# Rotating the sparse queries and keys: rows swapped by transfers within SBUF in place of a product with a permutation matrix

## The chip, the cores and the metric

The kernel runs on one core of a Trainium2 chip. The metric is the device time of one execution in microseconds (us), median over runs. Engines: PE is TensorE, DVE is VectorE, ACT is ScalarE, POOL is GpSimd, SP only issues transfers. Each engine works off its own queue in order, and engines wait for each other through semaphores.

## What is computed

A batch of 512 rows of width 1024 passes through two layers. The change lies in the second layer's sparse attention, whose heads are rotated in their first 16 of 64 dimensions:

```python
def partial_rope(x, cos, sin):
    xr = x[..., :ROT_DIM].astype(jnp.float32)
    x1, x2 = xr[..., :ROT_DIM // 2], xr[..., ROT_DIM // 2:]
    rot = jnp.concatenate([x1 * cos - x2 * sin, x2 * cos + x1 * sin], axis=-1)
    return jnp.concatenate([rot.astype(x.dtype), x[..., ROT_DIM:]], axis=-1)
...
    q = partial_rope(q.reshape(bsz, seq, A_HEADS, HEAD_DIM), cos, sin)
    k = partial_rope(k[:, :, None, :], cos, sin)[:, :, 0]
    qi = partial_rope(qi.reshape(bsz, seq, IDX_HEADS, IDX_DIM), cos, sin)
    ki = partial_rope(ki[:, :, None, :], cos, sin)[:, :, 0]
    a_out = dsa_attention(q, k, v, qi, ki, wi)
```

The index queries and keys (qi, ki) give a score for each pair of query and key; the top 128 keys of each query are kept, and softmax attention of the eight real heads (q, k, v) runs over those. Beside it in the same stage runs a convolution branch (four blocks of channels, 31 taps, layer norm). Then follow an output projection, cross attention and a feed-forward part.

## The kernel before

Every large product keeps single precision by splitting each operand into a high and a low part and adding three products (lines 385 to 387). A weight unit of 128 columns is loaded by SP into `raw`, its high part is cast on ACT (`whi`, line 361), its low part is subtracted on DVE in two halves (`wlo`, line 364), and PE then runs 24 products of 512 columns on it into a `ps_mm` buffer in PSUM, of which there are two. Three units fit into SBUF at a time.

Activations stand transposed: 128 head dimensions (two heads of 64) on the partitions, 512 rows along the free side. `roped_2` rotates such a tile: ACT copies it out of PSUM into `rx` (line 1527), PE multiplies `rx` by a constant permutation matrix `perm2` that exchanges rows 0 to 7 with rows 8 to 15 of each head (line 1529), DVE multiplies `rx` by the cosines (line 1530) and the permuted tile by the signed sines into `ry` (line 1532), adds both (line 1533), and `split` writes high and low part (`hl`, lines 409 and 410). `rx` and `ry` come from one ring of three buffers (tag `t2`), which other steps of the stage use too.

It is called eight times in `mix_2`, the stage of the change. First in `sparse_in`: index queries 0 and 1, and the index key (64 rows). From these PE computes the index scores (`scores_pair`, line 1518), ACT and DVE combine them into `acc` (lines 1486 to 1493), and DVE then runs the top-k: 48 rounds of MAX8 and MATCH_REPLACE8 (lines 1575 and 1576), each round on what the last one left. Meanwhile PE goes on with the units of the convolution branch (`conv_in`: pairs ua, ug), the convolution itself (line 1695), the key and value unit (`sparse_kv`, second rotation of 64 rows) and the four query units q0 to q3 (`sparse_q`, four rotations). The last part is `sparse_attend`: in steps of (block of 128 rows, pair of heads) PE does scores (line 1518), ACT exponentials (line 1606), PE transposes (line 1616) and products with the values (line 1629). Step (0, 0) needs q0, (0, 2) q1, (0, 4) q2 and (0, 6) q3; steps from (1, 0) on also need the masks of the top-k.

A scheduler that has its own estimate of every duration sets the order of each engine's queue from the order in which the program is written and from what would be ready. Only in `sparse_attend` with the end of the convolution branch is PE's order kept as written. So a change of one step moves others.

The first layer already has a rotation by transfers: `swap` (line 1501) exchanges halves of 32 rows with four transfers of 64 KB that ACT issues.

Of the kernel before, what the change touches and what calls it, by code (L numbers as in the profile page):

```python
# [20 lines left out]
F32 = mybir.dt.float32  # L21
# [3 lines left out]
OP = mybir.AluOpType  # L25
# [14 lines left out]
def _constants():  # L40
    p = np.arange(128)
    f = lambda a: np.asarray(a, np.float32)
    cols = {}

    def put(name, a):
        cols[name] = f(a).reshape(128, -1)

    put("ident", np.eye(128))
    put("i32", (p % 32)[:, None] == np.arange(32)[None, :])
    s, t = (p % 64)[:, None], np.arange(64)[None, :]  # L50
    put("maskS", np.concatenate([-f(t > s), t >= s], 1))
    put("maskY", np.broadcast_to((np.arange(128)[:, None] % 64) >= 32, (128, 32)))
    i, j = p[:, None], np.arange(128)[None, :]
    put("swm", np.concatenate([np.where(j > i, 0.0, NEG), np.where(j <= i, 0.0, NEG)], 1))
    put("bones", (i // 64) == (j // 64))
    put("hone", (i // 64) == np.arange(2)[None, :])
    m = p % 64
    put("perm2", (i == np.where(m < 8, p + 8, np.where(m < 16, p - 8, -1))[None, :]))
    h = np.arange(32, dtype=np.float32) / np.float32(32)
    inv1 = np.power(np.float32(10000.0), -h).astype(np.float32)  # L60
    g = np.arange(0, 16, 2, dtype=np.float32) / np.float32(16)
    inv2 = np.power(np.float32(500000.0), -g).astype(np.float32)
    put("inv", np.broadcast_to(np.concatenate([inv1, inv2]), (128, 40)))
    put("sgn1", np.where(m < 32, -1.0, 1.0))
    put("sgn2", np.where(m < 8, -1.0, np.where(m < 16, 1.0, 0.0)))
    put("rot2", m < 16)
    put("pass2", m >= 16)
    rm = np.ones((128, 8, 65))
    rm[:, :, 0] = 0
    put("rmask", rm)  # L70
    at, n = {}, 0
    order = [k for k in cols if k not in LATE] + [k for k in cols if k in LATE]
    for k in order:
        at[k] = (n, n + cols[k].shape[1])
        n += cols[k].shape[1]
    return at, np.ascontiguousarray(np.concatenate([cols[k] for k in order], 1))


LATE = ("maskS", "maskY", "bones", "rmask")
CAT, CONST = _constants()  # L80
NKEEP = CAT["maskS"][0]

# [148 lines left out]

PASS = 0.64

FILL = 32


class Builder:
# [20 lines left out]
    def setup_1(self):  # L258
        nc, I, cp = self.nc, self.I, self.cp
        self.mhalf = cp.tile([128, 16], F32, name="mhalf")  # L260
        nc.vector.memset(self.mhalf, -0.5)
        cp.tile([128, FILL], F32, name="fill")
        self.cst = cp.tile([128, NKEEP], F32, name="cst")
# [1257 lines left out]
    def roped_2(self, p, dst, ps, n, rows=None):  # L1521

        nc, V = self.nc, self.nc.vector
        C2, S2 = self.rot2
        rows = rows or 128
        x = p.tile([128, 512], F32, name="rx2", tag="t2", bufs=self.t2n)
        nc.scalar.copy(x[:rows], ps[:rows])
        pp = self.psum("at")
        nc.tensor.matmul(pp[:n], self.c("perm2")[:n, :n], x[:n], start=True, stop=True)
        V.tensor_tensor(x[:n], x[:n], C2[:n], op=OP.mult)  # L1530
        t = p.tile([128, 512], F32, name="ry2", tag="t2", bufs=self.t2n)
        V.tensor_tensor(t[:n], pp[:n], S2[:n], op=OP.mult)
        V.tensor_tensor(t[:n], x[:n], t[:n], op=OP.add)
        self.split(dst[0][:n], dst[1][:n], t[:n])
        return x
# [428 lines left out]
```

## Time and profile before

| | us |
|---|---|
| median of 3 runs | 1451.52 |
| lowest, highest | 1449.52, 1459.29 |
| the profiled execution's own time | 1450.54 |
| its span in the trace | 1448.8 |
| PE busy | 1407.9 (97%) |
| DVE busy | 870.5 (60%) |
| ACT busy | 557.9 (39%) |

The span runs from the first to the last recorded instruction; the execution's own time lies 1.7 us above it. Busy time of PE is modelled, since products overlap, and a busy PE may still run at the lower of its two clocks. The stage of the change lies between about 730 and 912 us of the span.

### The profile page before, as it was taken

The page shows a single profiled execution, that of the slowest core. Times are in us where ns is not written, and L with a number is a line of the kernel's source. Part 1 is how long each engine was busy: PE and PEld are TensorE (multiplying, and loading weights), DVE is VectorE, ACT ScalarE, POOL GpSimd, SP SyncE. Part 2 cuts the span into 40 slices and gives each one's busy share as a digit, 9 for nine tenths or more (in the row PEclk, how much of TensorE's full clock was granted, in tenths as well). Part 3 has the DMA queues.
Part 4 walks back from the last instruction along what each step waited for, and adds up shares of the span by engine and source line. Part 5 has one row for each costly group of instructions (what it writes and reads, how often), then busy time and mean ns, then how long its engine had stood idle before and what let it go on. Part 6 is the DMA issues. An engine that isn't in the chain of part 4 may idle for free.

```text
span 1448.8 us, 20320 instructions
## 1 busy us (share of the span) xinstructions
PE 1407.9 (97%) x7876; PEld 1113.7 (77%) x7876; DVE 870.5 (60%) x1983; ACT 557.9 (39%) x964; POOL 89.7 (6%) x164
## 2 busy tenths in 40 slices
PE   8799999999999999999999999999999999999998
PEld 6688768876776887887867556888888888888886
DVE  4768567776756775347569957465465555554232
ACT  4534345444344322333432126443344334343122
POOL 1101011201001000000001100000000000000000
PEclk9999999999999999999999998999999999999999
DMA  8367314422222441325226510252122332332221
GB/s 277 119 187 224 106 39 122 122 61 81 74 73 67 138 131 60 123 69 187 66 66 158 133 59 1 74 190 87 59 88 88 106 99 88 105 99 102 102 87 73
DMA packets 143617, 151.65 MB, mean 105 GB/s; under 512 B 22305, under 2 KB 118945, under 8 KB 143009
## 3 DMA queue, kind: packets, MB, share of 16 engines
q1 hardware_dynamic: 129088, 124.93, 27.6%
q0 software_dynamic: 4480, 14.98, 3.8%
q10 hardware_dynamic: 9952, 10.45, 2.2%
q8 instruction: 62, 1.02, 0.3%
q14 instruction: 35, 0.28, 0.1%
HBM read 135.33 MB, written 13.18 MB: 103 GB/s over the span
## 4 chain that ended last, share of the span: by engine, by line
PE 77%; DVE 8%; issue 2%; ACT 1%; POOL 1%; DMA 1%; ACTq 0%; POOLq 0%; DVEq 0%; SPq 0%
PE ps_mm L385 17%; PE ps_mm L386 17%; PE ps_mm L387 16%; DVE acc L1576 2%; PE ps_at L385 2%; PE ps_rw L385 2%; PE ps_at L387 2%; PE ps_at L386 2%; PE ps_rw L387 2%; PE ps_rw L386 2%; DVE m L1575 2%; DVE wlo L364 1%; PE ps_po L643 1%; PE ps_at L1518 1%; PE ps_at L614 1%
## 5 line engine op out<-in xcount | busy, mean ns | idle before, releaser
L364 DVE TENSOR_TENSOR wlo<-raw,whi 128x512 fp32r<-128x512 f32 x412 | 272.7, 683 | 279.4 <-ACT whi L361 276.1
L361 ACT CAST whi<-raw 128x1024 fp32r<-128x1024 f32 (+1 forms) x206 | 215.9, 1049 | 454.1 <-PE ps_mm L386 247.6
L386 PE MATMUL ps_mm<-blo,whi 128*128 128x512 f32 (+2 forms) x544 | 208.9, 384 | 0.0
L385 PE MATMUL ps_mm<-bhi,whi 128*128 128x512 f32 (+2 forms) x544 | 208.3, 383 | 0.0
L387 PE MATMUL ps_mm<-bhi,wlo 128*128 128x512 f32 (+2 forms) x544 | 207.6, 382 | 0.0
L385 PE MATMUL ps_mm<-hhi,whi 128*128 128x512 f32 (+1 forms) x488 | 195.2, 400 | 0.2 <-ACT hhi L409 0.2
L386 PE MATMUL ps_mm<-hlo,whi 128*128 128x512 f32 (+1 forms) x488 | 192.4, 394 | 0.8 <-DVE hlo L410 0.8
L387 PE MATMUL ps_mm<-hhi,wlo 128*128 128x512 f32 (+1 forms) x488 | 192.4, 394 | 0.0
L386 PEld LDWEIGHTS ps_mm<-blo,whi 128*128 128x128 f32 (+1 forms) x544 | 102.1, 188 | 22.9 <-issue 3.3
L385 PEld LDWEIGHTS ps_mm<-bhi,whi 128*128 128x128 f32 (+1 forms) x544 | 102.0, 188 | 21.5 <-issue 1.8
L387 PEld LDWEIGHTS ps_mm<-bhi,wlo 128*128 128x128 f32 (+1 forms) x544 | 102.0, 188 | 21.4 <-issue 1.8
L385 PEld LDWEIGHTS ps_mm<-hhi,whi 128*128 128x128 f32 x488 | 92.7, 190 | 20.4 <-issue 3.4
L387 PEld LDWEIGHTS ps_mm<-hhi,wlo 128*128 128x128 f32 x488 | 92.8, 190 | 18.2 <-issue 1.8
L386 PEld LDWEIGHTS ps_mm<-hlo,whi 128*128 128x128 f32 x488 | 92.7, 190 | 17.7 <-DVE hlo L410 1.3
L995 DVE TENSOR_TENSOR tmp<-U,L 32x31 f32<-32x31 f32 (+30 forms) x124 | 37.9, 306 | 4.2 <-DMA L<-lspill 2.0
L385 PE MATMUL ps_mm<-yhi,whi 128*128 128x512 f32 x96 | 39.1, 409 | 0.5 <-DVE ga L1183 0.3
L997 DVE TENSOR_TENSOR U<-U,tmp 32x31 f32<-32x31 f32 (+30 forms) x124 | 38.0, 306 | 2.3
L386 PE MATMUL ps_mm<-ylo,whi 128*128 128x512 f32 x96 | 38.7, 404 | 0.0
L387 PE MATMUL ps_mm<-yhi,wlo 128*128 128x512 f32 x96 | 38.3, 399 | 0.0
L421 ACT ACTIVATE nxs<-x 128x1024 f32<-128x1024 f32 x16 | 17.0, 1060 | 32.3 <-DVE x L1210 28.7
L1695 PE MATMUL ps_yk<-R,diag 128*32 128x512 f32 x256 | 29.3, 594 | 0.0
L385 PE MATMUL ps_mm<-mT,whi 128*128 128x256 f32 x96 | 28.0, 291 | 0.7 <-DVE kvt L410 0.6
(478 smaller groups left out, 2629.4 us busy)
## 6 DMA issues: line engine op xcount, KB each, us to landing
raw<-in_w_in_dram SPq DMA_DIRECT2D x24, 1024.0 KB, 5.3
raw<-in_w_in_dram SPq DMA_DIRECT2D x26, 512.0 KB, 3.9
raw<-in_w_gate_dram SPq DMA_DIRECT2D x11, 1024.0 KB, 5.1
raw<-in_w_up_dram SPq DMA_DIRECT2D x11, 1024.0 KB, 5.1
raw<-in_w_down_dram SPq DMA_DIRECT2D x10, 1024.0 KB, 4.9
raw<-in_w_out_dram SPq DMA_DIRECT2D x8, 1024.0 KB, 4.9
R<-cspill POOLq DMA_DIRECT2D x16, 270.0 KB, 6.0
raw<-in_w_k_cross_dram SPq DMA_DIRECT2D x4, 1024.0 KB, 7.8
```

The costliest lines, as they stand in the source:

```text
L361: nc.scalar.copy(h, v)
L364: self.last_lo = nc.vector.tensor_tensor(l[:, x], v[:, x], h[:, x].bitcast(F32), op=OP.subtract)
L385: mm(ps, L[0], R[0], start=first, stop=False)
L386: mm(ps, L[0], R[1], start=False, stop=False)
L387: mm(ps, L[1], R[0], start=False, stop=last)
L421: nc.scalar.activation(sc, x, AF.Square, accum_out=ss[:, 0:1])
L614: mm(pv[r][:, :n], q[64 * r:64 * r + 64, tb * 128:(tb + 1) * 128], kT[64 * r:64 * r + 64, key0:key0 + n], start=True, stop=True)
L995: V.tensor_tensor(t, U32[:np_, 0:a, m:m + 1].to_broadcast([np_, a, w]), L32[m // 16][:np_, m % 16:m % 16 + 1, m + 1:32].to_broadcast([np_, ...
L997: V.tensor_tensor(U32[:np_, 0:a, m + 1:32], U32[:np_, 0:a, m + 1:32], t, op=OP.add)
L1575: V.max(m, acc[tb][:, :n])
L1576: V.match_replace(acc[tb][:, :n], m, acc[tb][:, :n], DEAD)
L1695: nc.tensor.matmul(ps[32 * b:32 * b + 32], diag(i)[:, b * 8 + g, :], R[:, b, 4 * g:4 * g + 512], start=g == 0, stop=g == 7)
```

## The change

The permutation matrix is no longer among the constants, and a filler tile grows by its 128 columns so that all other tiles keep their places. In `roped_2` the product and its PSUM tile are gone. ACT issues three transfers for each head of 64 rows instead, from `rx` to `ry`: rows 8 to 15 to 0 to 7, rows 0 to 7 to 8 to 15, and rows 16 to 63 to the same place (the sines there are zero). So a call on 128 rows issues six transfers and a call on 64 rows three, 42 in all. The product with the sines now reads `ry` in SBUF, and stands ahead of the product with the cosines.

```diff
-    put("perm2", (i == np.where(m < 8, p + 8, np.where(m < 16, p - 8, -1))[None, :]))
...
-FILL = 32
+FILL = 160
...
         nc.scalar.copy(x[:rows], ps[:rows])
-        pp = self.psum("at")
-        nc.tensor.matmul(pp[:n], self.c("perm2")[:n, :n], x[:n], start=True, stop=True)
+        t = p.tile([128, 512], F32, name="ry2", tag="t2", bufs=self.t2n)
+        for h in range(0, n, 64):
+            for d, r, k in ((0, 8, 8), (8, 0, 8), (16, 16, 48)):
+                nc.scalar.dma_start(t[h + d:h + d + k], x[h + r:h + r + k])
+        V.tensor_tensor(t[:n], t[:n], S2[:n], op=OP.mult)
         V.tensor_tensor(x[:n], x[:n], C2[:n], op=OP.mult)
-        t = p.tile([128, 512], F32, name="ry2", tag="t2", bufs=self.t2n)
-        V.tensor_tensor(t[:n], pp[:n], S2[:n], op=OP.mult)
         V.tensor_tensor(t[:n], x[:n], t[:n], op=OP.add)
```

The queues are put in another order as well. In the changed kernel line numbers above 58 are one less. On PE, the first index score stood behind 24 products of the index key's unit, 20 of the convolution's and three permutation products; now it stands behind 24 and 79 products and no permutation product. The first convolution stands behind 137 products of the wide units before and behind 104 now.

ACT where the key and value unit (`rx_7348` before, `rx_7357` now) and q0 (`rx_7406`, `rx_7416`) are rotated, before:

```order
L1527 COPY rx_7348<-ps_mm 128x512
L361 CAST whi<-raw 128x1024
L409 CAST hl<-ry_7353 64x512
L361 CAST whi<-raw 128x1024
L1527 COPY rx_7406<-ps_mm 128x512
L409 CAST hl<-ry_7411 128x512
```

and now:

```order
L1526 COPY rx_7357<-ps_mm 128x512
L1530 DMA ry_7359<-rx_7357 8x512 x2
L1530 DMA ry_7359<-rx_7357 48x512
L360 CAST whi<-raw 128x1024
L1526 COPY rx_7416<-ps_mm 128x512
L408 CAST hl<-ry_7359 64x512
L1530 DMA ry_7418<-rx_7416 8x512 x2
L1530 DMA ry_7418<-rx_7416 48x512
```

The copy of q0 out of PSUM now stands ahead of the cast that ends the key's rotation, and q0's transfers (the last two rows, which stand twice) behind that cast. It goes on like this: each query's six transfers stand behind the cast that ends the rotation before it.

ACT at the last query (`rx_7551` before, `rx_7573` now), where `sparse_attend` begins with its exponentials (`ds`) and copies of transposes (`dPT`), before:

```order
L361 CAST whi<-raw 128x1024
L1527 COPY rx_7551<-ps_mm 128x512
L409 CAST hl<-ry_7556 128x512
L1606 ACTIVATE ds,dst<-ds,dst 128x128 x2
L1618 COPY dPT<-ps_rw 128x128
```

and now:

```order
L1530 DMA ry_7534<-rx_7532 48x512
L1526 COPY rx_7573<-ps_mm 128x512
L1606 ACTIVATE ds,dst<-ds,dst 128x128 x4
L1618 COPY dPT<-ps_rw 128x128
L408 CAST hl<-ry_7534 128x512
L1530 DMA ry_7575<-rx_7573 8x512 x2
L1530 DMA ry_7575<-rx_7573 48x512
```

The copy of q3 and the first exponentials now stand behind q2's transfers, and q3's transfers (again twice) behind the end of q2's rotation.

DVE at the end of the top-k, where it comes to the rotation of the key before:

```order
L1576 MATCH_REPLACE acc<-m_7275,acc 128x512
L1578 TENSOR_SCALAR acc<-acc 128x512
L1530 TENSOR_TENSOR rx_7348<-rx_7348,rp_6109 64x512
L1532 TENSOR_TENSOR ry_7353<-ps_at,rp_6109 64x512
L1562 COPY dV<-ps_at 128x256
L1533 TENSOR_TENSOR ry_7353<-rx_7348,ry_7353 64x512
```

and of q0 and q1 now:

```order
L1531 TENSOR_TENSOR ry_7418<-ry_7418,rp_6109 128x512
L1576 MATCH_REPLACE acc<-m_7284,acc 128x512
L1532 TENSOR_TENSOR rx_7416<-rx_7416,rp_6109 128x512
L1578 TENSOR_SCALAR acc<-acc 128x512
L1533 TENSOR_TENSOR ry_7418<-rx_7416,ry_7418 128x512
L363 TENSOR_TENSOR wlo<-raw,whi 128x512
L409 TENSOR_TENSOR hl<-ry_7418,hl 128x512
L363 TENSOR_TENSOR wlo<-raw,whi 128x512
L1531 TENSOR_TENSOR ry_7459<-ry_7459,rp_6109 128x512
L1532 TENSOR_TENSOR rx_7457<-rx_7457,rp_6109 128x512
```

The end of the top-k (the 512-wide TENSOR_SCALAR) now stands among the rotation of q0; the key's rotation stands six rounds of the top-k earlier.

## Rows read from the trace of the kernel before

**Rows 1.** The page: the line of busy times by engine, and the shares of the chain that ended last.

```profile
PE 1407.9 (97%) x7876; PEld 1113.7 (77%) x7876; DVE 870.5 (60%) x1983; ACT 557.9 (39%) x964; POOL 89.7 (6%) x164
...
PE 77%; DVE 8%; issue 2%; ACT 1%; POOL 1%; DMA 1%; ACTq 0%; POOLq 0%; DVEq 0%; SPq 0%
```

**Rows 2.** Stretches of 10 us and, for the transfers alone, two of 2 us: length, busy us of PE, PEld, DVE, ACT and POOL (instructions), granted clock of PE, share of the 16 DMA engines, GB/s.

```profile
810.00:820.00 10.00, 10.00 (x78) 4.23 (x77) 9.73 (x20) 0.31 (x1) 2.74 (x5) 1.00 0.47 161
820.00:830.00 10.00, 8.94 (x39) 6.14 (x37) 9.66 (x21) 2.33 (x4) 0.00 (x0) 1.00 0.42 85
830.00:840.00 10.00, 8.38 (x30) 4.78 (x31) 6.24 (x11) 3.72 (x6) 0.00 (x0) 0.83 0.42 131
860.00:870.00 10.00, 7.29 (x40) 4.05 (x40) 7.87 (x37) 4.63 (x19) 0.56 (x1) 0.76 0.00 0
870.00:880.00 10.00, 9.81 (x54) 6.61 (x52) 5.08 (x24) 6.23 (x21) 0.00 (x0) 0.50 0.01 2
880.00:890.00 10.00, 9.74 (x78) 6.63 (x76) 7.36 (x29) 6.26 (x20) 0.55 (x1) 0.89 0.00 1
...
834.00:836.00 2.00, 2.00 (x9) 1.61 (x8) 1.72 (x3) 0.21 (x1) 0.00 (x0) 0.89 1.01 341
856.00:858.00 2.00, 2.00 (x10) 1.66 (x9) 1.28 (x3) 0.62 (x1) 0.00 (x0) 1.00 0.83 259
```

**Rows 3.** The timeline of PE: start us, us, engine, line, what, and in brackets the idle time before it with what ended it.

```profile
732.11 1.02 PE L1529 MATMUL ps_at<-rx,cst 128*128 128x512 f32 x2
...
745.63 0.38 PE L1518 MATMUL ps_at<-hl 64*128 64x256 f32 x1
...
828.55 0.39 PE L385 MATMUL ps_mm<-bhi,whi 128*128 128x512 f32 x1
831.62 2.07 PE L1529 MATMUL ps_at<-rx,cst 128*128 128x512 f32 x2 [2.69 <-ACT rx L1527]
...
847.31 0.39 PE L386 MATMUL ps_mm<-blo,whi 128*128 128x512 f32 x1
...
853.46 0.39 PE L386 MATMUL ps_mm<-blo,whi 128*128 128x512 f32 x1
...
858.98 0.60 PE L1732 MATMUL ps_yk<-cst,cv 128*128 128x128 f32 x4
860.53 1.12 PE L1529 MATMUL ps_at<-rx,cst 128*128 128x512 f32 x2 [0.95 <-ACT rx L1527]
...
867.93 0.58 PE L1518 MATMUL ps_at<-hl 64*128 64x256 f32 x1
```

**Rows 4.** The timeline of ACT, same columns.

```profile
729.55 0.59 ACT L1527 COPY rx<-ps_mm 128x512 f32<-128x512 f32 x1 [4.05 <-PE ps_mm L387]
732.24 1.05 ACT L361 CAST whi<-raw 128x1024 fp32r<-128x1024 f32 x1 [2.10 <-PE ps_mm L386]
...
803.62 0.69 ACT L1701 ACTIVATE cv<-ps_yk,par 128x512 f32<-128x512 f32 x1 [7.26 <-PE ps_yk L1695]
...
819.69 0.69 ACT L1701 ACTIVATE cv<-ps_yk,par 128x512 f32<-128x512 f32 x1 [11.19 <-PE ps_yk L1695]
...
829.53 0.62 ACT L409 CAST hl<-ry 64x512 fp32r<-64x512 f32 x1 [7.67 <-DVE ry L1533]
830.05 1.04 ACT L361 CAST whi<-raw 128x1024 fp32r<-128x1024 f32 x1
831.00 0.57 ACT L1527 COPY rx<-ps_mm 128x512 f32<-128x512 f32 x1
```

**Rows 5.** The timeline of DVE, same columns.

```profile
747.61 0.35 DVE L1489 TENSOR_SCALAR acc<-rel,wi 128x256 f32<-128x256 f32 x1 [2.03 <-ACT rel L1486]
...
824.71 0.68 DVE L1576 MATCH_REPLACE8 acc<-m,acc 128x512 f32<-128x512 f32 x1
825.42 0.69 DVE L1575 MAX8 m<-acc 128x8 f32<-128x512 f32 x1
826.15 0.09 DVE L1576 MATCH_VALUE_LOAD acc<-m,acc 128x8 f32 x1
826.23 0.67 DVE L1576 MATCH_REPLACE8 acc<-m,acc 128x512 f32<-128x512 f32 x1
826.94 0.43 DVE L1578 TENSOR_SCALAR acc<-acc 128x512 f32<-128x512 f32 x1
827.28 0.68 DVE L1530 TENSOR_TENSOR rx<-rx,rp 64x512 f32<-64x512 f32 x1
827.88 0.68 DVE L1532 TENSOR_TENSOR ry<-ps_at,rp 64x512 f32<-64x512 f32 x1
```

**Rows 6.** Transfers that ACT and SP already issue between tiles of SBUF: the first layer's `swap` (issues on ACT's queue with min, median and max ns, first and last start; then its time to landing; then four issues in a row in ACT's timeline), and the copy of a finished key to the other 64 partitions (engine, KB each, median us to landing).

```profile
L1501 ACTq DMA_DIRECT2D ry<-rx x20: 514/602/626, 217.0 to 289.5; - x20
DMA to landing us min/median/max: 2.0/3.5/5.5
...
277.65 2.47 ACTq L1501 DMA_DIRECT2D ry<-rx  x4
...
hl<-hl SPq DMA_DIRECT2D x4, 128.0 KB, 2.2
```

## The prediction

> **What bounds the kernel now.** I read the page first: PE is busy for 97% of the span and carries 77% of the chain that ended last, DVE 8% [rows 1]. So a change pays when it takes work or waits from PE's queue, and only as long as PE is what the end waits for. Then the stretches of the stage [rows 2]: from 810 us on DVE is the second full engine (9.73 and 9.66 of 10 us, the top-k), PE is full until about 828, then has gaps in 820 to 840 and in 860 to 870, and its granted clock falls from 1.00 (2.4 GHz) to 0.83 and 0.76 on average in two of these stretches and to 0.50 (1.2 GHz) throughout 870 to 880. Last the three timelines, for what ended each gap. PE stands 2.69 us before 831.62, until ACT has copied q0 out of PSUM [rows 3]; ACT did that only at 831.00, behind the key's cast, which had waited 7.67 us for DVE [rows 4], since DVE reaches the key's rotation only when the top-k ends at 827.4 [rows 5]. The second such wait is 0.95 us before 860.53 [rows 3].
>
> **What goes.** Eight permutation products of 1.02 us each [rows 3] are 8.2 us of PE; seven of them lie before the last weight product at 858.98, that is 7.1. The 2.69 us wait goes with them, since PE no longer needs `rx`, only the buffer in PSUM, and q0's copy now stands ahead of the key's cast. If that gap goes, the clock's fall behind it goes too: 0.17 of the 10 us at 830, 1.7 us [rows 2]. Together 11.5 us. So PE should finish its weight products earlier; whether the end comes earlier hangs on the rotations.
>
> **What comes.** 42 issues on ACT. The nearest row is `swap`: 0.60 us each, and four in a row took 2.47 [rows 6], so six hold ACT's queue for 3.6 us and three for 1.8. Landing is bounded by 2.2 us (a finished key, quiet queues) and 3.5 (median of `swap`, worst 5.5) [rows 6]; the pieces here are of 16 and 96 KB on either side of `swap`'s 64, and I take 3.0. From the first of six issues to the last landing that is 5 x 0.60 + 3.0 = 6.0 us, of three 4.2. A permutation product brought the same rows in 1.02. On DVE a rotation keeps its three operations, 0.6 us from start to start [rows 5]. The freed PSUM tile and the smaller load of constants I cost at nothing: neither is waited for here.
>
> The Trainium skill (DMA: Bandwidth & Descriptors, Anatomy of one DMA) fits a transfer, on the path that POOL issues, as about 2.0 us fixed and little for the bytes. For 96 KB that is an estimate of 2.2 us instead of my 3.0, and at two links of the chain below, where landing decides, the sum would come out 1.6 us lower. The finished key's 2.2 agrees; `swap`'s median speaks for more.
>
> **The start of the stage.** The copy at 729.55 [rows 4] is followed by six issues, 730.1 to 733.7; they land at 736.1. The second query's copy ends at 734.4. The cast that ends the first rotation stands behind a weight cast that waits until PE is through with the index key, 737.9 (24 products of some 0.23 us behind 732.3, without a permutation product between them); so it ends at 739.4, and the second six issues run until 743.0. Only then is the key copied out of PSUM, 743.6. PE needs that buffer at 743.5: 0.5 us lost. The second rotation ends at 748.5 on ACT, the key's three transfers land at 752.7, and its cast waits behind another weight cast (1.05 us [rows 4]) for PE until 756.3. PE reaches the first index score behind 103 products at about 757.0, and finds the key just ready. Before, it was at 745.63 [rows 3]. So the scores, and with them the top-k, start 11.4 us later, on a DVE that has no room: from the first `acc` at 747.61 to the end of the top-k at 827.3 it took 79.7 us [rows 5]. Inside that stretch now stand six more operations of the rotations and the key's value copy, and two others fewer (one of `u`, one of `wlo`): 2.7 us more. From 758.8 that gives **841.3 for the end of the top-k**, 14 us later than before.
>
> **PE's way.** A weight product takes 0.228 us (27 of them between 847.31 and 853.46 [rows 3]); a convolution is what two of them leave between 803.62 and 819.69 [rows 4] less 39 products: 7.2. The index scores take what 745.63 to 803.62 leaves behind 155 products and two convolutions, 8.3. From 757.0: the scores and 25 products to 771.0, then three convolutions, 112 products to the end of the key's unit at 818.1 (before about 820.0), its transposes 0.4, 48 products for q0 and q1 to 829.5, the fourth convolution, q2 and q3: **PE is through at 847.6**, against 858.98.
>
> **The seam is what decides.** The key's rotation fits in between rounds: DVE comes to it six rounds of 1.5 us [rows 5] and ten operations of about 0.6 ahead of its later end, at 827, its cast ends at 830.8, and q0's issues run to 834.4 and land at 836.8. But DVE ends q0's rotation only behind the top-k: 841.9, its cast on ACT 842.5. From there each query waits for the one before it, since its six issues stand in ACT's queue behind that cast. One link is 6.0 us to landing, then on DVE the three operations and a `wlo` half in between (2.5), then the cast: 9.2 us. q1's cast ends at 851.7, and its issues hold the copy of q3 out of PSUM until 855.9: step (0, 2) needs that buffer, so PE does it at 856.0. q2's cast ends at 860.7 (DVE is at it from 858.3, behind a copy of a transpose, so here landing at 857.7 does not decide), q3's at 869.2, and its low part at 869.9. PE makes step (0, 6) at 870.0. Before it was at 867.93 [rows 3]. So of the 11.4 us that PE was ahead nothing is left: **2.1 us later**. PE stands nearly idle for 20 us, and what is behind the seam is unchanged.
>
> **Sum.** 1450.5 for the profiled execution becomes 1452.6. That execution is 1.0 us under the median of the runs shown, 1451.52, so the prediction for the median is 1453.5, no change. I count over 1% (14.5 us) as a change, about what can be told in this kernel.
>
> **Bounds of the forecast.** Landing at 2.2 us in two links: 1.6 less. At 3.5: 1.0 more. The clock: before, it was back at 2.4 GHz at about 882 (a mean of 0.89 over 880 to 890 is 2.2 us at half), 14 us behind step (0, 6), and PE was full in that time; at 830 a mean of 0.83 is 3.4 us at half. If it returns that soon, up to 4.5 us come back: 0.9 us in each of the five steps between, in which ACT has room (6.23 of 10 us busy in 870 to 880 [rows 2]). Stalls I may have missed at the start, where ACT is held by issues and the 512-wide index scores stand behind a weight cast: up to 3 us more. So 1446 to 1459 for this case alone, and I give it 0.62.
>
> **Rivals.**
>
> *The gain stays* (0.13). If the top-k were not last, or a link took under 6 us, step (0, 6) would come 15 to 20 us after q3's product as a matter of PE and not of transfers, and most of the 11.5 us would be kept: 1441, and 1437 with the clock back early. Against it: the link without any landing is already 3.6 of issues, 2.5 of DVE and a cast, 6.8 us, and three of them behind 842.5 give 863, so it needs an earlier end of the top-k too. For it: I have put the index scores 11.4 us later by a walk with several waits that just meet.
>
> *Landing as slow as its worst* (0.15). The loads of weights take all 16 DMA engines in stretches (1.01 at 834, 0.83 at 856 [rows 2]), and `swap` has landed after 5.5 us. 2.5 more in each of three links: 7.5, so 1461; with a late start 1465.
>
> *The clock stays down* (0.10), the rival that ends slower. Before, gaps of 2.7 us within 860 to 870 were followed by 1.2 GHz until about 882 [rows 2]. Now PE has nearly no work from 848 to 870. If it then stays at 1.2 GHz for the steps of the blocks (2, .) and (3, .) too, where it was busy for 9.74 of 10 us [rows 2], each 10 us of them costs up to that: over the 30 us up to 912 as much as 29 us, and 1472 when two thirds of it take effect. It decides from 15 us more at the lower clock than before. Against it: the same dense steps brought the clock back before.
>
> The Trainium skill (TensorE: Matmul & The Clock Gate, HAM oscillation) warns of just this: an array that waits for transfers again and again is slowed again and again. By that rule the 1472 of this rival holds if the gaps repeat; my walk has three of them at the seam, none behind it, and the fall in 860 to 880 agrees with the rule.
>
> That the change does not do what it says is excluded by PE's queue, which holds no permutation product any more.
>
> **How the numbers follow.** Faster by over 1% (under 1437) is the lower end of the first rival: 0.05. Slower by over 1% (over 1466) is the clock's rival, and a little of slow landing: 0.11. The rest, 0.84, is no change. The range of 8 in 10 takes in the forecast, most of the kept gain's upper part and slow landing: 1443 to 1465.
>
> **What would show it.** In the changed trace: 42 issues of about 0.6 us on ACT's queue, landing 2 to 3.5; the first index score near 757; the end of the top-k near 841, 14 us later; PE's weight products of the queries through at about 848, with no wait for a copy near 830; casts of the queries' rotations about 9 us apart; step (0, 6) near 870, and a low clock there. I am wrong if the top-k ends before 835 or if the casts are 6 us apart (then it is faster), or if the clock is still 0.50 behind 890 (then it is slower).

## The result, and the profile after

The changed kernel takes 1462.45 us (median of 9 runs, 1460.78 to 1468.31) against 1451.92 for the kernel before on the same chip: a ratio of 1.0068, 95% interval 1.0046 to 1.0089. That is 6.7 to 12.9 us slower. It lies within 1%, and within the range of the prediction, but the forecast was 2 us, so about 8 us are to be explained.

The profiled execution took 1468.31 us. It is 8.7 us later already at the copy of `rx` that begins the stage (738.27 now, 729.55 before [rows 4]), ahead of the first rotation, and the profiles of this study begin the stage anywhere between 729.55 and 743.64. So **all times below that are called "after the start" are counted from that copy**; on that count the first index score was at 16.1 before, the end of the top-k at 97.8 and step (0, 6) at 138.4.

On the page PE's busy time is about what it was [rows 1]. Its share of the chain that ended last reads 40%, beside 77% before, but the two cannot be compared: this chain is followed back only to 735.22, half of the span, and its shares add up to 50%.

```profile
PE 1411.2 (96%) x7860; PEld 1119.9 (76%) x7860; DVE 870.3 (59%) x1983; ACT 557.5 (38%) x964; POOL 90.1 (6%) x164
...
PE 40%; DVE 6%; ACT 1%; issue 1%; ACTq 1%; DMA 1%; POOLq 0%; POOL 0%; DVEq 0%
```

The stretches of the stage, columns as in [rows 2] (length, busy us of PE, PEld, DVE, ACT, POOL, granted clock of PE, share of the DMA engines, GB/s):

```profile
758.00:768.00 10.00, 10.00 (x44) 7.64 (x43) 6.48 (x11) 3.60 (x6) 2.81 (x5) 1.00 0.83 221
768.00:778.00 10.00, 6.80 (x23) 3.96 (x21) 1.33 (x4) 1.16 (x4) 0.00 (x0) 0.66 0.53 116
778.00:788.00 10.00, 10.00 (x29) 5.92 (x30) 7.24 (x20) 4.71 (x9) 0.56 (x1) 0.50 0.00 1
...
868.00:878.00 10.00, 2.91 (x14) 1.69 (x14) 7.49 (x25) 3.51 (x12) 0.93 (x1) 0.61 0.39 133
878.00:888.00 10.00, 4.92 (x26) 2.77 (x26) 4.72 (x19) 2.85 (x12) 0.00 (x0) 0.50 0.09 25
888.00:898.00 10.00, 9.81 (x54) 6.53 (x52) 5.49 (x24) 5.84 (x18) 0.00 (x0) 0.50 0.00 1
```

There are two stretches of low clock. The one at the seam (868 to 898) was expected. The other, 768 to 788, was not: there PE makes the index scores. Before, it did so at 1.00, with no wait above 0.3 us (stretches of the kernel before):

```profile
740.00:750.00 10.00, 10.00 (x43) 6.20 (x41) 5.62 (x10) 3.46 (x6) 0.00 (x0) 1.00 0.50 129
750.00:760.00 10.00, 9.72 (x46) 6.21 (x46) 8.32 (x24) 4.96 (x11) 0.00 (x0) 1.00 0.20 54
```

PE's timeline now, columns as in [rows 3], tells what ended its gaps:

```profile
765.71 0.38 PE L1517 MATMUL ps_at<-hl 64*128 64x256 f32 x1
766.92 0.49 PE L1517 MATMUL ps_at<-hl 64*128 64x256 f32 x2
772.06 1.01 PE L1517 MATMUL ps_at<-hl 64*128 64x256 f32 x4 [3.05 <-DMA hl<-hl]
...
884.72 0.58 PE L1517 MATMUL ps_at<-hl 64*128 64x256 f32 x1 [5.08 <-ACT hl L408]
```

The first index score comes at 27.4 after the start, where the walk of the prediction has it (757.0, which is 27.4 after 729.55). It and the two behind it use the key on partitions 0 to 63. Those of the other head use the copy of the key on partitions 64 to 127, and PE stands 3.05 us for that. The chain of waits (start, us, what) has the copy on the path:

```profile
765.65 6.28 DMA hl<-hl
772.06 1.01 PE ps_at L1517 x4
```

6.28 us from issue to landing, for two transfers that landed after 2.2 before [rows 6]. What the engines of the transfers did meanwhile is in stretches of 2 us, and by queue over 764 to 774 (queue: packets, MB, share of the packets' time; by the bytes, q0 is POOL's and q1 SP's):

```profile
764.00:766.00 2.00, 2.00 (x9) 1.31 (x7) 0.86 (x2) 1.95 (x3) 1.08 (x2) 1.00 1.15 337
766.00:768.00 2.00, 2.00 (x9) 1.34 (x9) 1.10 (x3) 0.49 (x2) 0.00 (x0) 1.00 1.03 216
768.00:770.00 2.00, 1.01 (x5) 0.49 (x3) 0.28 (x1) 0.00 (x0) 0.00 (x0) 1.00 1.03 203
770.00:772.00 2.00, 0.00 (x0) 0.00 (x0) 0.00 (x0) 0.00 (x0) 0.00 (x0) 0.82 1.09 216
772.00:774.00 2.00, 1.94 (x6) 1.25 (x6) 0.00 (x0) 0.00 (x0) 0.00 (x0) 0.50 0.54 160
```

```profile
q0 software_dynamic: 320, 1.11, 49.8%
q1 hardware_dynamic: 1908, 1.14, 46.4%
```

The 16 engines are full from 764 to 772 (shares of 1.03 to 1.15). Half of the traffic is POOL's, and POOL's timeline names it: the four loads of the first convolution's input `R` (270 KB each), issued 2.8 us ahead of the key's copy.

```profile
760.05 0.59 POOL L1676 DMA_DIRECT2D cspill<-u  x1 [30.30 <-issue]
762.87 2.21 POOL L1680 DMA_DIRECT2D R<-cspill  x4 [2.22 <-DMA cspill<-u]
```

Before, the same loads came 21 us *behind* the key's copy; POOL's and SP's timelines of the kernel before:

```profile
766.10 2.22 POOL L1680 DMA_DIRECT2D R<-cspill  x4 [2.42 <-DMA cspill<-u]
```

```profile
744.89 1.25 SPq L1510 DMA_DIRECT2D hl<-hl  x2
```

After the start the key's copy moved from 15.3 to 27.4 and the loads from 36.6 to 24.6, and the two met. It took both moves: at their old place the loads would have come 9 us behind the key's copy. They follow the convolution's products, and of these 79 now stand ahead of the first index score in PE's queue, where 20 stood.

At the seam, ACT's timeline has the casts of q0 to q3 and the issues between them:

```profile
859.48 0.62 ACT L408 CAST hl<-ry 128x512 fp32r<-128x512 f32 x1 [3.92 <-DVE ry L1533]
859.54 3.82 ACTq L1530 DMA_DIRECT2D ry<-rx  x6
...
868.16 0.62 ACT L408 CAST hl<-ry 128x512 fp32r<-128x512 f32 x1 [1.39 <-DVE ry L1533]
...
876.41 0.62 ACT L408 CAST hl<-ry 128x512 fp32r<-128x512 f32 x1 [2.06 <-DVE ry L1533]
...
884.04 0.62 ACT L408 CAST hl<-ry 128x512 fp32r<-128x512 f32 x1 [2.74 <-DVE ry L1533]
```

The links are 8.7, 8.3 and 7.6 us, and they begin where DVE ends the top-k, at 858.85:

```profile
858.43 0.42 DVE L1578 TENSOR_SCALAR acc<-acc 128x512 f32<-128x512 f32 x1
```

That is 120.6 after the start, against 97.8 before and the 111.8 of the prediction. Step (0, 6) is at 146.5: 8.1 us later than before.

### The profile page after: what moved, and what is told of

Its sections match the earlier page's. It is cut to its first block, busy times and chain, and to the rows that moved or that the text cites. A ratio compares the mean times of both kernels' runs of the same rounds, so it can differ in the third digit from the quotient of the medians.

```text
span 1466.5 us, 20361 instructions
## 1 busy us (share of the span) xinstructions
PE 1411.2 (96%) x7860; PEld 1119.9 (76%) x7860; DVE 870.3 (59%) x1983; ACT 557.5 (38%) x964; POOL 90.1 (6%) x164
## 4 chain that ended last, share of the span: by engine, by line
PE 40%; DVE 6%; ACT 1%; issue 1%; ACTq 1%; DMA 1%; POOLq 0%; POOL 0%; DVEq 0%
PE ps_mm L385 8%; PE ps_mm L386 8%; PE ps_mm L384 8%; DVE acc L1576 2%; DVE m L1575 2%; PE ps_rw L384 1%; PE ps_at L384 1%; PE ps_at L386 1%; PE ps_at L385 1%; PE ps_rw L386 1%; PE ps_rw L385 1%; PE ps_at L1517 1%; ACTq L1530 1%; PE ps_po L1629 1%; PE ps_yk L386 1%
## 5 line engine op out<-in xcount | busy, mean ns | idle before, releaser
L1517 PE MATMUL ps_at<-hl 64*128 64x256 f32 (+2 forms) x84 | 25.7, 488 | 13.3 <-ACT hl L408 10.1
L1517 PEld LDWEIGHTS ps_at<-hl 64*128 64x128 f32 x84 | 15.6, 265 | 22.4 <-ACT hl L408 11.4
```

The costliest lines, as they stand in the source:

```text
L1517: self.nc.tensor.matmul(pss[r][:, :n], q[a][c, tb * 128:(tb + 1) * 128], k[b][c, :n], start=i == 0, stop=i == 2)
```

## The experiments

**Theory A**: the loss begins at the key's copy. It lands late, PE stands 3 us, the clock falls for 17 us, the scores and with them the top-k come late, and the seam's chain starts late. **Theory B**: the seam's chain of transfers costs the loss by itself. The readings of all runs first; "clock" is the time at 1.2 GHz in and behind the index scores, worked out from the granted clock of the stretches ((1 - clock) x length / 0.5), the times are after the start, each ratio is to the kernel before on the same chip.

| kernel | wait for the key's copy | clock | end of top-k | step (0, 6) | median | ratio [95%] |
|---|---|---|---|---|---|---|
| before | none | 0 | 97.8 | 138.4 | 1451.92 | |
| change | 3.05 | 17 | 120.6 | 146.5 | 1462.45 | 1.0068 [1.0046, 1.0089] |
| e1 key copied by ACT | none | 0 | 108.4 | 136.6 | 1450.92 | 0.9985 [0.9964, 1.0006] |
| e2 copy on ACT's queue | 3.57 | 7 | 120.5 | 145.5 | 1460.95 | 1.0066 [1.0044, 1.0088] |
| e3 queries and kv only | none | 0 | 98.0 | 138.5 | 1454.48 | 1.0012 [0.9993, 1.0032] |
| e4 index part only | 3.64 | 14 | 124.6 | 145.6 | 1458.17 | 1.0031 [1.0009, 1.0054] |
| e5 gap filled | 3.67 | 17 | 123.4 | 154.3 | 1468.87 | 1.0109 [1.0084, 1.0133] |
| e6 e1 + more buffers | none | 0 | 109.3 | 134.8 | 1452.47 | 0.9997 [0.9983, 1.0012] |
| e7 e6 + four issues | none | 0 | 108.4 | 136.0 | 1460.15 | 1.0026 [1.0002, 1.0051] |
| e8 e1, index part only | none | 0 | 111.2 | 135.4 | 1453.53 | 0.9990 [0.9963, 1.0018] |
| e9 convolution's loads later | none | 0 | 112.3 | 138.4 | 1456.90 | 1.0016 [0.9991, 1.0041] |
| e10 gap filled in order | 0.36 | 10 | 117.6 | 149.4 | 1465.94 | 1.0086 [1.0053, 1.0118] |
| e11 e6, q2 and q3 by product | none | 0 | 109.3 | 131.5 | 1445.85 | 0.9941 [0.9921, 0.9962] |
| e12 e10 with 128 rows | none | 0 | 113.7 | 143.0 | 1463.20 | 1.0057 [1.0030, 1.0084] |

Medians of one kernel move by 2 us from chip to chip, and single executions differ by 10 us and more, largely ahead of the stage; the ratios and the times after the start are what is compared.

**e1: the key's second half by ACT.**

```diff
-        self.both_halves(kiT)
+        self.both_halves(kiT, True)
...
         for t in kT:
+            if eng:
+                self.nc.scalar.copy(t[64:128], t[0:64])
+                continue
             self.nc.sync.dma_start(t[64:128].bitcast(F32), t[0:64].bitcast(F32))
```

> The index key's second half (partitions 64 to 127) is written by two more copies on ACT instead of two transfers on SP's queue; all rotations stay with transfers. Times counted from the copy of rx that begins the stage; in the changed kernel there: first index score 27.4, end of the top-k 120.6, step (0, 6) 146.5; before: 16.1, 97.8, 138.4. Theory A (most of the loss begins at this copy: it lands 6.3 us after its issue, PE stands 3.05 us and the granted clock is 0.50 for the following 16 us): the wait of 3 us is gone, the clock in the index scores stays at 1.00, the scores are through about 8 us earlier, the top-k ends at 111 to 113, step (0, 6) at 138 to 140, the time is 1453 to 1456. Theory B (the four queries' chain of transfers at the seam costs the loss by itself, wherever the top-k ends): 1460 to 1463, no change against the changed kernel. Theory C (the clock falls there anyway, since PE has other gaps): the wait goes but the clock in the scores is still under 0.7, and the time is 1458 to 1461.

ACT's timeline has the two copies, and the stretch of the scores is full and at 1.00:

```profile
758.08 1.14 ACT L1510 CAST hl<-hl 64x512 fp32r<-64x512 f32 x2
```

```profile
760.00:770.00 10.00, 9.96 (x49) 6.60 (x49) 8.97 (x24) 5.88 (x12) 0.00 (x0) 1.00 0.37 86
```

The wait and the low clock are gone, the top-k ends 12.2 us earlier than in the changed kernel and step (0, 6) comes 9.8 earlier, both by more than Theory A gave. One reason is another order of PE's queue: 11 weight products stand among the index scores here, 19 in the changed kernel, so not all of the 12.2 is the wait and the clock. The ratio to the kernel before falls from 1.0068 to 0.9985; the two intervals are apart. Theory B falls: all eight rotations and the seam's chain are unchanged here. So does Theory C of the expectation, that the clock falls there anyway. The seam still waits for transfers (casts of q0 to q3 at 111.4, 120.1, 128.3, 136.0).

**e2: the queue or the engines?**

```diff
-        self.both_halves(kiT)
+        self.both_halves(kiT, self.nc.scalar)
```

> The same two transfers of the index key, issued on ACT's queue and not on SP's, where five loads of weights had been issued ahead of them. If they were late because they stood behind those loads in SP's queue: landing 2 to 3.5 us, PE's wait under 1 us, top-k end 112 to 115 after the stage's first copy and 1453 to 1457. If they were late because the loads fill the 16 engines, whatever the queue: landing 5 us or more, a wait of 2 us or more, the clock down as in the changed kernel, 1460 to 1463.

On ACT's own queue the copy takes no less time; the chain has it with 7.26 us:

```profile
762.04 7.26 DMA hl<-hl
```

So it was not the place in SP's queue. The Trainium skill (DMA: Bandwidth & Descriptors, Queues, rings and completion order) says that SP and ACT have a ring each on the same 16 engines and no engines of their own; 7.26 beside 6.28 agrees. The clock was low for only 7 us here, and the scores were through at 47.0 after the start, 1.7 earlier than in the changed kernel, yet the top-k ended no earlier. PE resumed the scores 1.0 us later, three weight products stand earlier among them, and DVE began the top-k at 43.5 where it began at 40.7; so this run does not divide the loss.

**e3 and e4: one half of the change each** (the other half by products as before; `by` chooses in `roped_2`).

```diff
-            self.roped_2(p, qiT[a], ps, 128)
+            self.roped_2(p, qiT[a], ps, 128, by=False)
...
-        x = self.roped_2(p, kiT, ps, 64, 68)
+        x = self.roped_2(p, kiT, ps, 64, 68, by=False)
```

> Transfers only for the key/value unit and the four queries; the index queries and the index key are rotated by products again. Theory A: index scores, clock and top-k are as before (first score about 16 after the stage's first copy, end of the top-k about 98); the seam's chain starts there, with the key's cast at about 103, q0's at 112 and links of about 8.7 us, so q3's cast at about 138 and step (0, 6) at 139 to 140: 1451 to 1455. Theory B (the seam's chain costs the loss by itself): 1459 to 1463.

> The other half: transfers only for the index queries and the index key; the key/value unit and the four queries by products. Theory A: the key's copy is late again (wait of about 3 us, clock 0.50 to 0.6 in the scores), the top-k ends at 119 to 121 after the stage's first copy; with products at the seam the queries follow faster, q2's copy waits for the top-k's end, step (0, 6) at 137 to 142: 1451 to 1457. Theory B: as before, 1450 to 1453, although the top-k is late.

e3 has step (0, 6) at 138.5, as before, though five products are gone: the top-k ends at 98.0, and the chain behind it (q0's cast at 113.2, links of 8.7, 8.2 and 7.7) eats what PE gained. So the seam gives the gain back and costs no more. e4 has the late copy, the low clock and step (0, 6) 7.2 later than before. At that step the index part alone makes nearly the whole loss of 8.1. The time shows less of it: a ratio of 1.0031 beside 1.0068, with intervals that just overlap, and a median 1 us above what was expected. The step came 3.6 us behind what was expected; PE waits there for copies of `rx` for 3.9 us, much as in the kernel before (3.6).

**e9: the convolution's loads out of the way.** Everything stays with transfers, the key's copy on SP's queue; two tiny copies on POOL make the first convolution's loads wait for it.

```diff
         self.both_halves(kiT)
+        self.kiT = kiT
...
+            if i == 0:
+                for c in (0, 64):
+                    nc.gpsimd.tensor_copy(R[c:c + 64, 0, 0:1], self.kiT[1][64:128, 0:1].bitcast(F32))
             for s in range(4):
```

> The changed kernel, key copied by SP's transfers as there, but the first convolution's four loads (R, 270 KB each, issued by POOL at 24.6 to 26.8 after the stage's first copy, just ahead of the key's copy at 27.4) wait on POOL until that copy has landed. If those 1.08 MB were what held the key's copy up: it lands 2.2 to 4 us after its issue, PE's wait is under 1 us, the clock stays 1.00 in the index scores, the top-k ends at 108 to 111, step (0, 6) comes at 136 to 139, 1450 to 1454. If the loads of weights alone hold it up: landing 5 us or more, a wait of 2 to 3 us, the clock at 0.50 behind it, 1460 to 1464.

SP's and POOL's timelines: the key's copy is issued at 763.02 and POOL has it at 766.34, 3.3 us later; the loads follow.

```profile
763.02 1.33 SPq L1510 DMA_DIRECT2D hl<-hl  x2
```

```profile
766.34 0.42 POOL L1681 COPY R<-hl 64x1 f32<-64x1 f32 x2 [8.31 <-DMA hl<-hl]
766.96 2.21 POOL L1684 DMA_DIRECT2D R<-cspill  x4 [0.21 <-POOL R L1681]
```

No wait of PE for the key, the clock 1.00, step (0, 6) at 138.4 as before. The ratio 1.0016 is no difference from before that could be told; the median, 1456.90, is above what was expected, and the top-k ended 1.3 us behind it. So those four loads are what held the copy up, and moving them alone takes most of the loss away.

This run also divides the loss, since PE's queue has the same products in the same order around the scores as in the changed kernel. PE's first and last group of scores behind the key's copy, first of e9, then of the changed kernel (its first group, at 772.06, is shown above):

```profile
766.32 0.63 PE L1518 MATMUL ps_at<-hl 64*128 64x256 f32 x4
...
774.61 1.11 PE L1518 MATMUL ps_at<-hl 64*128 64x512 f32 x6
```

```profile
785.35 1.65 PE L1517 MATMUL ps_at<-hl 64*128 64x512 f32 x6
```

In e9 these scores begin at 30.7 after the start and take 9.4 us; in the changed kernel they begin at 33.8 and take 14.9. So the wait cost 3.1 us and the low clock 5.5, together 8.6. The top-k's end moved by 8.3. On DVE, from its first operation on the scores to the end of the top-k, the same operations stand in both: 77.4 us of work in 82.7 in e9, 77.7 in 90.9 in the changed kernel.

**e5, e10, e12: the wait or the clock?** Spare products, whose result is not used, keep PE busy until the key's copy lands. e5 failed: only 10 of 28 stood ahead of the wait, which remained (3.67 us, clock 0.50 for 17 us).

> The changed kernel with 28 spare products of 512 columns on the first half of the index key (6.4 us of PE, result unused) queued between the first index score and the second, so that PE works while the key's copy is on its way. Times from the copy of rx that begins the stage. In the changed kernel the second index score comes at 33.8, the top-k ends at 120.6; with the key copied by ACT 28.6 and 108.4, so the wait alone explains 5.2 of the 12.2 us. Theory A1 (the other 7 us are the clock at 0.50 behind the gap): no wait over 1 us, clock 1.00 through the scores, end of the top-k at 113 to 115, step (0, 6) at 141 to 143, 1453 to 1457. Theory A2 (the clock has no part in it, and the spare products only take PE's time): end of the top-k at 120 or later, 1461 to 1466.

In e10 all 28 stand ahead of it, each on 64 rows of the array; in e12 27 of them use 128:

```diff
-                                for _ in range(28):
-                                    mm(pf, qiT[0][0][0:64, 0:128], kiT[0][0:64, :], start=True, stop=True)
+                                mm(pf, qiT[0][0][0:64, 0:128], kiT[0][0:64, :], start=True, stop=False)
+                                for k in range(27):
+                                    mm(pf, qiT[0][0][:, 0:128], qiT[0][0], start=False, stop=k == 26)
```

> As the run with the gap filled, but with all 28 spare products (6.4 us) queued ahead of the first index score that needs the key's second half; there only 10 stood ahead of it, and PE still waited 3.67 us. Theory A1 (most of the loss is the clock behind the gap): wait under 1 us, clock 1.00 in the scores, end of the top-k at 113 to 116 (the key's landing is 5.2 later than with the copy by ACT, whose top-k ended at 108.4), step (0, 6) at 141 to 144, 1454 to 1458. Theory A2 (the wait by itself): end of the top-k at 119 or later, 1461 or more.

> As the run with the gap filled in order, where the clock fell to 0.50 from about 770.7 to 781 although PE was busy and waited only 0.36 us; there all 28 spare products used 64 of the array's 128 rows. Here 27 of the 28 use all 128 rows (first index query by itself), so only their rows differ. If the clock fell there because the spare products use half of the array: the clock stays at 1.00 through the scores, the top-k ends at 112 to 115 after the stage's first copy (117.6 there, 120.6 in the changed kernel, 108.4 with the key copied by ACT), step (0, 6) 3 to 5 us earlier than its 149.4, 1458 to 1463; the 12.2 us between the changed kernel and the key by ACT are then 5 of landing and 7 of clock. If the scores themselves, or the wait of 0.4 us, take the clock down: again 0.50 for about 10 us, end of the top-k at 117 to 118, 1464 to 1468.

The stretches behind the spare products, first of e10, then of e12:

```profile
766.00:768.00 2.00, 2.00 (x11) 1.62 (x10) 0.00 (x0) 0.00 (x0) 0.00 (x0) 1.00 1.06 198
768.00:770.00 2.00, 1.54 (x8) 0.86 (x8) 0.00 (x0) 0.00 (x0) 0.00 (x0) 1.00 0.82 205
770.00:772.00 2.00, 2.00 (x12) 1.31 (x10) 0.97 (x2) 0.66 (x2) 0.00 (x0) 0.63 0.03 9
```

```profile
772.00:774.00 2.00, 2.00 (x11) 1.65 (x10) 0.00 (x0) 0.00 (x0) 0.00 (x0) 1.00 1.09 214
774.00:776.00 2.00, 2.00 (x13) 1.35 (x11) 0.00 (x0) 0.14 (x1) 0.00 (x0) 1.00 0.55 152
776.00:778.00 2.00, 1.95 (x10) 1.22 (x9) 1.48 (x4) 1.40 (x4) 0.00 (x0) 1.00 0.02 4
```

In e10 the clock fell for 10 us although PE shows busy, and neither theory's numbers came: the top-k's end, 117.6, lies between them. In e12, whose queue is the same but for those rows, the clock stayed at 1.00 and the top-k ended at 113.7, within what was expected; the time, 1463.2, lies just above the upper edge. PE took the key's copy no earlier than in the changed kernel (33.8): at 34.8 in e10, at 35.0 in e12. Up to the top-k's end DVE has the same operations in e1, e10 and e12. So 113.7 - 108.4 = 5.3 us remain with the late landing and no low clock, and 117.6 - 113.7 = 3.9 are what 10 us of low clock cost in e10, with the wait of 0.36 us. Of the 120.6 - 113.7 = 6.9 to the changed kernel DVE's idle time makes 5.0 (13.3 us against 8.3 in the stretch that was counted for e9); the rest is three operations that stand behind the top-k's end in e12. That is near the 5.5 of e9. The time of the whole kernel does not show it here: e12 is as slow as the changed kernel, and its spare products take 6.4 us of PE, more than the wait they fill.

**e6, e7, e8, e11: a version that beats both kernels?** With e1 as the base the seam is what waits for transfers. e6 takes `ry` of q0 and q1 out of the ring of three buffers:

```diff
+        self.dPT = p.tile([128, 4, 512], F32, name="dPT")
...
-                self.roped_2(p, qT[-1], ps, 128)
+                self.roped_2(p, qT[-1], ps, 128, t=self.dPT[:, {0: 3, 1: 0}[u], :] if u in {0: 3, 1: 0} else None)
```

> The kernel with the key copied by ACT (top-k end 108.4 after the stage's first copy, casts of the queries 111.4, 120.1, 128.3, 136.0, step (0, 6) about 136.7), where ry of q0 and q1 lies in two slots of the later dPT tile and not in the ring of three. If the ring sets the links of 8.7 us at the seam: q0's six issues run before the top-k's end, the casts of q0 and q1 come at about 110 and 114, q2's at about 124, q3's at 133, step (0, 6) at 133 to 134, 3 us earlier: 1446 to 1449. If ACT's issues and the landing set them whatever the ring: casts still 8 us or more apart, 1450 to 1453.

The casts came at 109.9, 114.7, 126.5 and 134.1: q0 and q1 as expected, so the ring did set those links. q2 and q3 came 2.5 and 1.1 us behind what was expected: q2's copy out of PSUM, and with it its issues, still stands in ACT's queue behind the cast that ends q1's rotation. Step (0, 6) is 1.9 us earlier than in e1, which the time doesn't show.

e7 also replaces two of six transfers by a second copy out of PSUM (`nc.scalar.copy(t[:n], ps[:n])`).

> As the one with more buffers, and rows 16 to 63 of each head come by a second copy out of PSUM on ACT (0.6 us), so that a call on 128 rows issues four transfers of 16 KB instead of six (2.5 us of issues for 3.8) and a call on 64 rows two. If issues on ACT are what is left at the seam: each link 0.7 us shorter, at the stage's start too (the two queries' copies 4.5 us apart become about 3.8), step (0, 6) 1 to 2 us earlier than there: 1444 to 1448. If PE's own products bound the seam by then: within 1 us of the one with more buffers.

The links are 5.5, 11.1 and 7.3 us beside 4.8, 11.8 and 7.6 in e6, not 0.7 shorter each. At the stage's start the first index score comes 1.2 us earlier, but PE stands for 2.0 and 1.4 us that it did not stand before. The longer of these waits (waited for: us, times, longest):

```profile
PE ps_mm L384 <- ACT ry L1531: 2.0, 1, 2.0
```

The second copy keeps the PSUM buffer, and PE waits for that. Step (0, 6) is 1.2 us later than in e6, and the median, 1460.15, lies above both readings: the expectation failed.

> Transfers only for the index queries and the index key, whose second half is copied by ACT; the key/value unit and the four queries by products. Index scores and top-k as in the kernel with the key copied by ACT (first score 27.4, no wait, top-k's end 107 to 110). If the seam's chain of transfers costs more than the five products (5.1 us of PE) it saves: PE through with its weight products at about 126, step (0, 6) 132 to 135, 1446 to 1449. If not: step (0, 6) at 137 or later, 1451 to 1454.

e8 (index part by transfers, the rest by products) has step (0, 6) at 135.4, 1.2 earlier than e1 and just behind what the first reading gave. The time, 1453.53, lies in the range of the second, but its interval takes in part of the first too, so it does not decide.

> The kernel with more buffers (key copied by ACT, ry of q0 and q1 outside the ring), and q2 and q3 rotated by products again. PE's weight products end at about 120 after the stage's first copy. If the links of transfers behind the top-k are what the seam still waits for: casts of q2 at about 121 and q3 at about 126 (128.3 and 136.0 with the key copied by ACT alone), step (0, 6) at 126 to 128, and from the stage's first copy to the end of the span 708 to 712 us (before 719.3, key by ACT 716.1): 1442 to 1447, faster than both kernels. If PE's clock takes it back: 1449 to 1452.

e11 is e6 with q2 and q3 by products (`by=u < 2`). ACT's timeline at the seam:

```profile
853.61 0.62 ACT L409 CAST hl<-dPT 128x512 fp32r<-128x512 f32 x1 [5.09 <-DVE dPT L1544]
858.47 0.62 ACT L409 CAST hl<-dPT 128x512 fp32r<-128x512 f32 x1 [3.57 <-DVE dPT L1544]
859.94 0.58 ACT L1530 COPY rx<-ps_mm 128x512 f32<-128x512 f32 x1
863.79 0.62 ACT L409 CAST hl<-ry 128x512 fp32r<-128x512 f32 x1 [3.27 <-DVE ry L1544]
```

The casts are at 110.0, 114.8, 120.2 and 128.4, step (0, 6) at 131.5, later than the 126 to 128 expected, since q3's product stands ahead of all steps in PE's queue and PE waited 3.1 and 0.95 us for copies of `rx`. The ratio is 0.9941 [0.9921, 0.9962]: 0.4 to 0.8% faster than the kernel before, and its interval lies below that of the changed kernel too. It lies below that of e6 as well, which differs only in q2 and q3. So transfers pay less than products for the last two queries, which have no other work to land behind. What the kernel before would gain from the key copied by ACT alone was not run; how much of the 0.4 to 0.8% is the transfers' is not shown.

## Why the prediction was right and where it failed

- **What goes** was right. There is no permutation product and no wait for a copy near 830, and behind the scores the clock stays at 1.00 until the seam. In e9, where the key is not late, PE is through with its weight products at 118.2 after the start (predicted 118.1, as 847.6); in the changed kernel itself at 127.5.
- **The price of a transfer** was near: issues of 0.63 us (median of 42; 0.60 taken), six in 3.8 to 4.5 us, landing at the seam 2.3 us (last issue 879.7, DVE goes on at 882.0; 3.0 taken). The estimate of 2.2 from the fit of the Trainium skill (DMA: Bandwidth & Descriptors, Anatomy of one DMA) was the better one there. The 6.28 of the key's copy, with all engines full, is far from such a fit.
- **The start of the stage** was right up to the first index score. **The step that failed is "finds the key just ready"**: ready was only the half on partitions 0 to 63. The two transfers that bring the other half got no landing of their own in the walk. With the 2.2 us of [rows 6] they would have been there when PE wanted them, at 769.0 (772.06 less the wait). What had to be asked is which transfers the later key would meet: the loads of `R` were in the trace, and the key was forecast 11 us later, behind 79 of the convolution's products, which bring those loads forward. The two met, and the copy took 6.28 us.
- **The clock in the scores** was the second part of the miss. The prediction had weighed gaps and low clock only near 830 and at the seam. A wait of 3.1 and a clock that cost 5.5 us put the top-k's end at 120.6 where 111.8 was forecast; e9, without both, has it at 112.3.
- **"Given back at the seam"**, the likeliest case, was right as a mechanism: links of 8.7, 8.3, 7.6 (forecast 9.2, 9.0, 8.5), e3 with step (0, 6) where it was before, and e9, where the key lands as quickly as the walk needs, has step (0, 6) at 138.4 (forecast 140.5) and a ratio of 1.0016 beside the forecast's 1.0014. That the forecast of no change held for the changed kernel too is luck in part: the miss of 8 us was smaller than the 1% that counts as a change.
- **The rivals.** *Landing as slow as its worst* had the right time, 1461 to 1465, from 2.5 us more in each of three links at the seam. That is not what happened: the seam's links were no longer than forecast, and one copy at the start was 4 us late and counted for more through the clock. So the right time came from the wrong place. *The clock stays down*: at the seam it was low for about 31 us (868 to 908) against 17 before, close to the 15 us more that were set as the deciding point, and it came back at about 901, some 2 us behind the 890 that was named as a sign of being wrong (on the count of the kernel before). But from step (0, 6) to the end of the span the kernel needs 581.8 us now and 580.9 before, so behind that step this cost 1 us, not 18; ahead of it PE was mostly idle (7.8 of the 20 us from 868 to 888 busy). *The gain stays* did not come. The Trainium skill (TensorE: Matmul & The Clock Gate, HAM oscillation) warns that waits for transfers slow the array down; the fall behind the 3.05 us wait agrees, at a place where I had not looked.

## What to carry to other kernels

A step that becomes later takes its transfers with it: list which other transfers will be under way at the new time, on every queue, before taking a landing time from a quiet stretch. A wait of PE of 3 us cost some 5 more at the end of the top-k through the clock behind it, so a gap that is new in a dense stretch is to be priced with the stretch that follows. A product that is replaced by transfers pays only where the landing is hidden; at the end of a chain a product of 1 us is cheaper than 6 us of issues and landing.

## What was unexpected of the hardware

- The granted clock fell to 0.50 for 10 us in e10 behind 28 products on 64 rows of the array, with PE shown as busy and a wait of 0.36 us, and stayed at 1.00 in e12, where 27 of them used 128 rows. Whether the rows alone make the difference, or the short wait too, was not tried.
- Two transfers of 128 KB within SBUF landed after 2.2 us in a quiet stretch and after 6.28 us (SP's queue) and 7.26 us (ACT's) beside the four loads of 270 KB that POOL had issued and a load of weights.
- ACT wrote 64 partitions from the other 64 in two copies of 1.14 us together, less than the quiet transfers took.
